# Attention values with a high|low stationary operand, and probabilities normalised before they are turned

## The chip, the cores and the metric

One NeuronCore of a Trainium2 chip runs the whole program. The metric is the device time of one execution in microseconds (us). The engines are PE (matmuls; PEld is its weight load), DVE (VectorE), ACT (ScalarE), POOL (GpSimd) and SP (DMA queues). Each works through its own instructions in order, and semaphores join them.

## What is computed

A network in float32 over 256 latent and 256 context tokens, 1024 features wide. The first block has two layers, each a mixer (attention beside a state-space scan, SSD) and a feed-forward part; layer 0 also updates the context, layer 1 only the latents. The second block has a layer of sparse attention by an index (DSA) with a feed-forward part, and a layer with three attention branches (NSA: compressed keys, selected blocks, a window) with eight experts. The attention of the first block reads:

```python
def one_block(q_blk):
    s = jnp.einsum('bqkgd,bskd->bkgqs', q_blk, k).astype(jnp.float32) * scale
    p = jax.nn.softmax(s, axis=-1).astype(v.dtype)
    return jnp.einsum('bkgqs,bskd->bqkgd', p, v)
```

Heads have 64 features; in the first block 8 query heads share 2 key heads, in the second 16 share 4. DSA and NSA add masks, and NSA adds up its branches, each times a gate by token and head. The attended heads, beside the scan's output in the first block, go through an output projection.

## The kernel before

The program is one long stream: the first block's layers, then DSA, then NSA. Linear layers hold each operand as a high part and a rest, both float32r, and add three products (`mm3`, L369 to L371; the weights are split by ACT at L363 and DVE at L364). Features lie along the partitions of `hT` and `mixT` (two parts, high and low), 128 tokens to a tile. A scheduler orders each engine's instructions by priority, and the written order sets the priority; pools of tiles with a fixed number of buffers (`bank("tr", 2)` for transposes, `bank("o", 2)` for the attention's outputs, `wk` for work tiles) add waits.

Attention goes by groups of one token tile (L627 to L672): 1 head with 512 keys, 2 heads with 256, or 4 heads with 128. Layer 0 has 24 groups (16 of 512 keys, 8 of 256), layer 1 has 16 of 512, DSA 12 (4 of 128 keys, 8 of 256), NSA 24 (8 of 128, 16 of 256) and four compressed steps. A group has three steps:

- `scores`: the matmuls against the keys (L643, L644; L639 adds a mask), DVE's maximum (L647), ACT's Exp with the row sums (L652), one for each head.
- `turn`: four transposes of the probabilities on PE (L660) and one copy out of PSUM (`evac`, two of three by ACT at L130, one by DVE at L132).
- `values`: float32 matmuls (L670) with the turned probabilities of 128x128 as stationary operand and 64 columns of V moving. Their output has tokens along the partitions, eight heads of 64 in one bank.

After eight heads DVE takes the reciprocal of the row sums and multiplies the bank by it (`heads_out`, L1245; in NSA also the gates, and L1248 and L1249 add the branches). `to_mixT` then turns the 512 features with four transposes (L680), DVE copies them out (L685), ACT casts the high part (L691) and DVE subtracts (L692). A block of eight heads and one token tile is a job; there are four in layer 0, two in layer 1, four in DSA and four in NSA: 14.

`pipeline(units, (1, 2))` writes the steps of DSA and NSA so that a group's `turn` comes one group after its `scores`, its `values` two more after that, and what follows `values` with it. In the mixers the groups are merged with the scan and the convolutions. In NSA the compressed branch (`compressed`) has its own scores (L1562, L1563), and its values are one float32 matmul of 512 columns (L1582) against a block-diagonal `vbd` that DVE makes at the entry by four products of 128x256 (L1503).

## Time and profile before

| | us |
|---|---|
| median of 3 runs | 2746.94 |
| lowest and highest | 2740.97, 2750.49 |
| the profiled execution | 2753.68 |
| its span in the trace | 2751.8 |
| PE busy | 2644.2 (96%) |
| DVE busy | 2100.7 (76%) |
| ACT busy | 1529.1 (56%) |
| POOL busy | 52.7 (2%) |

The granted TensorE clock over the span is 0.978 of full speed. The attention stages lie at about 100 to 267 us (layer 0), 830 to 916 (layer 1), 1230 to 1272 (DSA) and 1591 to 1680 (NSA). A busy share is an average over the span, so a stage is read from its own window. Ends of matmuls are modelled: what a matmul costs PE is read from one start to the next.

### The profile page before, as it was taken

What the parts mean: (1) busy time and instruction counts of PE and PEld (TensorE: products, weight loads), DVE (VectorE), ACT (ScalarE), POOL (GpSimd) and SP (SyncE); (2) the same over time, 40 slices, a digit from 0 to 9 for tenths busy, and PEclk for the clock granted to TensorE, in tenths of its full rate; (3) what the DMA queues carried; (4) which work ended last, traced back from release to release, by engine and by line L of the source; (5) the groups of instructions that cost most, each with busy time, mean ns of one, the idle gap of its engine ahead of it and who ended that gap; (6) DMA issues with size and microseconds to landing.
All of it is one profiled execution on the core that took longest, in us unless ns stands there. A gap on an engine that the chain in (4) does not pass through costs nothing. (4 is left out here: it accounts for less than half of the span.)

```text
span 2751.8 us, 37805 instructions
## 1 busy us (share of the span) xinstructions
PE 2644.2 (96%) x13941; PEld 2178.2 (79%) x13941; DVE 2100.7 (76%) x2818; ACT 1529.1 (56%) x2259; POOL 52.7 (2%) x103
## 2 busy tenths in 40 slices
PE   7999999999999899999999999999999999999998
PEld 4877777778777799778997888788888888787876
DVE  5777667566687777576765866899989898888887
ACT  4444532223554444465444654777777777777775
POOL 0011000000001000000000000000000000000000
PEclk9999999999999999999999998999999999999999
DMA  6321667776531388442875623899999999999996
GB/s 240 118 93 32 214 201 249 256 261 212 160 114 39 100 300 281 150 140 92 277 243 168 207 75 126 292 336 345 338 336 340 345 335 343 350 345 347 349 340 239
DMA packets 180264, 641.87 MB, mean 233 GB/s; under 512 B 20621, under 2 KB 21351, under 8 KB 180071
## 3 DMA queue, kind: packets, MB, share of 16 engines
q1 hardware_dynamic: 177840, 636.05, 66.4%
q10 hardware_dynamic: 2231, 3.33, 0.4%
q8 instruction: 111, 1.82, 0.3%
q14 instruction: 82, 0.67, 0.1%
HBM read 638.25 MB, written 1.05 MB: 232 GB/s over the span
## 5 line engine op out<-in xcount | busy, mean ns | idle before, releaser
L363 ACT CAST hl<-raw 128x1024 fp32r<-128x1024 f32 (+3 forms) x1010 | 1025.4, 1033 | 647.5 <-PE mm L371 391.1
L364 DVE TENSOR_TENSOR hl<-raw,hl 128x1024 fp32r<-128x1024 f32 (+3 forms) x1010 | 1184.2, 1200 | 204.3 <-ACT hl L363 198.8
L370 PE MATMUL mm<-hl,h 128*128 128x512 f32 (+4 forms) x1616 | 631.5, 391 | 4.0 <-DVE hl L364 3.1
L371 PE MATMUL mm<-hl,h 128*128 128x512 f32 (+4 forms) x1616 | 626.3, 388 | 0.0
L369 PE MATMUL mm<-hl,h 128*128 128x512 f32 (+4 forms) x1616 | 623.8, 389 | 1.1 <-DVE wk L1160 0.8
L369 PE MATMUL mm<-h,hl 128*128 128x256 f32 (+1 forms) x1208 | 394.5, 327 | 6.0 <-DVE hl L364 5.9
L370 PE MATMUL mm<-h,hl 128*128 128x256 f32 (+1 forms) x1208 | 391.2, 324 | 0.0
L371 PE MATMUL mm<-h,hl 128*128 128x256 f32 (+1 forms) x1208 | 390.9, 324 | 0.0
L370 PEld LDWEIGHTS mm<-hl,h 128*128 128x128 f32 x1616 | 304.8, 189 | 77.9 <-DVE hl L364 13.3
L369 PEld LDWEIGHTS mm<-hl,h 128*128 128x128 f32 x1616 | 304.9, 189 | 69.8 <-ACT hl L363 3.0
L371 PEld LDWEIGHTS mm<-hl,h 128*128 128x128 f32 x1616 | 304.8, 189 | 61.4
L296 DVE SCALAR_TENSOR_TENSOR mv<-mv,st 128x1024 f32<-128x1024 f32 x154 | 196.5, 1283 | 109.9 <-DMA mv<-in_w_ada_dram 76.0
L369 PEld LDWEIGHTS mm<-h,hl 128*128 128x128 f32 x1208 | 228.2, 189 | 35.1 <-DVE hl L364 10.8
L371 PEld LDWEIGHTS mm<-h,hl 128*128 128x128 f32 x1208 | 228.0, 189 | 21.1 <-issue 1.7
L370 PEld LDWEIGHTS mm<-h,hl 128*128 128x128 f32 x1208 | 228.2, 189 | 20.5 <-issue 1.7
L370 PE MATMUL o<-hl,h 128*128 128x512 f32 x480 | 191.5, 399 | 1.4 <-DVE hl L364 0.2
L371 PE MATMUL o<-hl,h 128*128 128x512 f32 x480 | 189.1, 394 | 0.0
L369 PE MATMUL o<-hl,h 128*128 128x512 f32 x480 | 178.9, 399 | 0.0
L370 PEld LDWEIGHTS o<-hl,h 128*128 128x128 f32 x480 | 90.3, 188 | 24.7 <-DVE hl L364 4.4
L369 PEld LDWEIGHTS o<-hl,h 128*128 128x128 f32 x480 | 90.2, 188 | 20.7 <-issue 0.8
L371 PEld LDWEIGHTS o<-hl,h 128*128 128x128 f32 x480 | 90.3, 188 | 19.6
L652 ACT ACTIVATE wk<-mm,nmx 128x256 f32<-128x256 f32 (+2 forms) x144 | 69.1, 491 | 55.6 <-DVE nmx L647 55.4
(448 smaller groups left out, 2801.4 us busy)
## 6 DMA issues: line engine op xcount, KB each, us to landing
raw<-in_moe_w_up_dram SPq DMA_DIRECT2D x221, 512.0 KB, 5.4
raw<-in_moe_w_gate_dram SPq DMA_DIRECT2D x220, 512.0 KB, 5.5
raw<-in_moe_w_down_dram SPq DMA_DIRECT2D x219, 512.0 KB, 5.2
mv<-in_w_ada_dram SPq DMA_DIRECT2D x96, 512.0 KB, 4.9
mv<-in_w_mod_dram SPq DMA_DIRECT2D x85, 512.0 KB, 4.6
raw<-in_w_gate_dram SPq DMA_DIRECT2D x44, 512.0 KB, 4.8
raw<-in_w_up_dram SPq DMA_DIRECT2D x44, 512.0 KB, 4.6
raw<-in_w_down_dram SPq DMA_DIRECT2D x44, 512.0 KB, 3.6
```

The costliest lines, as they stand in the source:

```text
L296: nc.vector.scalar_tensor_tensor(acc, raw, st[:, k, cnd:cnd + 1], acc, op0=ALU.mult, op1=ALU.add)
L363: self.in_turn("hi", lambda: nc.scalar.copy(hl[:, 0], raw), after and after[0])
L364: self.in_turn("lo", lambda: nc.vector.tensor_sub(hl[:, 1], raw, hl[:, 0]), after and after[1])
L369: nc.tensor.matmul(out, s[1], m[0], start=start, stop=False)
L370: nc.tensor.matmul(out, s[0], m[1], start=False, stop=False)
L371: nc.tensor.matmul(out, s[0], m[0], start=False, stop=stop)
L652: nc.scalar.activation(pr[:, j * nk:(j + 1) * nk], sb[:, j * nk:(j + 1) * nk], AF.Exp, bias=nmx[:, j:j + 1], accum_out=sm[:, g + j:g + j + 1])
```

## The change

V is stored once as a high part and a rest side by side, 64 + 64 columns of float32r (`vS`, made by `put_values`: ACT casts, DVE subtracts). This pair is now the stationary operand. The probabilities are normalised straight after the Exp: DVE takes the reciprocal of the row sums (and in NSA multiplies it by the gates, which are made ready once), and ACT scales each head by it (L667), or GpSimd all four heads where there are 128 keys (L663). After the transposes ACT casts the high part (L679) and DVE subtracts the rest (L680). The matmuls (L689) let the two parts of the probabilities move past V's pair, 256 columns at a time (512 where there are 128 keys). The output has features along the partitions: the rows of V's high part and those of its rest, which `heads_to_mixT` adds for four heads at a time (ACT copies at L703 and L704, DVE adds at L705 and L706, ACT casts at L708, DVE subtracts at L709). The transposes and copies of `to_mixT` go for attention, as do `heads_out` and the norms.

A job now fills two banks "o" of four heads each where it filled one of eight; in NSA all branches add into these two in PSUM, from the compressed values to the last branch. The compressed values are eight matmuls of 128 columns against `vst`, made by four products of 128x512. The lag is (2, 2), and in layer 1 `n_head` is 5 where it was 7.

```diff
+    def put_values(self, dst, src):
+        self.nc.scalar.copy(dst[:, :, 0], src)
+        self.nc.vector.tensor_sub(dst[:, :, 1], src, dst[:, :, 0])
...
+            nc.vector.reciprocal(sm, sm)
+            if coef is not None:
+                nc.vector.tensor_mul(sm, sm, coef[:, g:g + hb])
+            if hb > 2:
+                nc.gpsimd.tensor_mul(pr.rearrange("p (h k) -> p h k", h=hb), pr.rearrange("p (h k) -> p h k", h=hb),
+                                     sm.unsqueeze(2).to_broadcast([128, hb, nk]))
+            else:
+                for j in range(hb):
+                    nc.scalar.activation(pr[:, j * nk:(j + 1) * nk], pr[:, j * nk:(j + 1) * nk], AF.Copy, scale=sm[:, j:j + 1])
 
         def turn():
...
-            pt = self.wk(512)
-            self.evac(pt[:, :hb * nk], tb[:, :hb * nk])
-            st["pt"] = pt
+            if g % vb == 0:
+                sh["pT"] = pool.tile([128, 2, nkt, vb, 128], F32R, name="pT", bufs=2)
+            src = tb.rearrange("p (h k n) -> p k h n", h=hb, k=nkt)
+            hi, lo = (sh["pT"][:, i, :, g % vb:g % vb + hb] for i in range(2))
+            st["pT"] = sh["pT"]
+            nc.scalar.copy(hi, src)
+            nc.vector.tensor_sub(lo, src, hi)
 
         def values():
-            pt, ob = st["pt"], o_of()
-            for j in range(hb):
-                for kt in range(nkt):
-                    c = (j * nkt + kt) * 128
-                    nc.tensor.matmul(ob[:, (g + j) * 64:(g + j + 1) * 64], pt[:, c:c + 128],
-                                     v_of(g + j, kt), start=(kt == 0), stop=(kt == nkt - 1))
+            if (g + hb) % vb:
+                return
+            g0 = g + hb - vb
+            out = o_of(g0)[:, (g0 % 4) * 128:(g0 % 4 + vb) * 128]
+            for kt in range(nkt):
+                for i in (1, 0):
+                    nc.tensor.matmul(out, v_of(g0, kt), st["pT"][:, i, kt].rearrange("p h n -> p (h n)"),
...
+    def heads_to_mixT(self, mixT, k0, t, ob):
...
+        nc.scalar.copy(s[lo], ov[hi, :, 0])
+        nc.scalar.copy(s[hi], ov[lo, :, 1])
+        nc.vector.tensor_add(f[lo], ov[lo, :, 0], s[lo])
+        nc.vector.tensor_add(f[hi], ov[hi, :, 1], s[hi])
+        h, l = (mixT[:, i, k0:k0 + 2, t * 128:t * 128 + 128] for i in range(2))
+        nc.scalar.copy(h, f)
+        nc.vector.tensor_sub(l, f, h)
...
-            n_head = 7 if last else 5
+            n_head = 5
...
-            self.pipeline(units, (1, 2))
+            self.pipeline(units, (2, 2))
...
+                    v2 = self.wk(2, 64).bitcast(F32R)
+                    nc.scalar.copy(v2[:, 0], b[:, h * 64:h * 64 + 64])
+                    nc.vector.tensor_sub(v2[:, 1], b[:, h * 64:h * 64 + 64], v2[:, 0])
+                    nc.vector.tensor_mul(vst[:, h], v2.bitcast(F32).rearrange("p a d -> p (a d)").unsqueeze(1).to_broadcast([128, 4, 128]),
+                                         rowm.unsqueeze(2).to_broadcast([128, 4, 128]))
...
                         def values():
-                            ob = self.bank("o", 2)
-                            nc.tensor.matmul(ob, st["pT"], vbd[:, hf], start=True, stop=True)
...
+                            for g in range(2):
+                                for h in range(4):
+                                    nc.tensor.matmul(o_of(4 * g)[:, h * 128:h * 128 + 128], vst[:, 2 * hf + g, h], st["pT"][:, g],
+                                                     start=(h == 0), stop=False, skip_group_check=True)
```

On ACT, in the second half of DSA (groups of 256 keys; `wk` are probabilities, `tr` the transposed ones in PSUM, `h` is `mixT`), before:

```order
L652 ACTIVATE wk,sums<-mm,nmx 128x256 x2
L130 COPY wk<-tr 128x512
L652 ACTIVATE wk,sums<-mm,nmx 128x256 x2
L130 COPY wk<-tr 128x512
L691 CAST h<-wk 128x4x128
L652 ACTIVATE wk,sums<-mm,nmx 128x256 x4
L691 CAST h<-wk 128x4x128
L130 COPY wk<-tr 128x512
```

and after, where `psum` holds the reciprocals, `pT` the turned parts and `o` the output bank:

```order
L704 COPY wk<-o 64x256
L657 ACTIVATE wk,psum<-mm,nmx 128x256 x2
L708 CAST h<-wk 128x2x128
L667 ACTIVATE wk<-wk,psum 128x256
L679 CAST pT<-tr 128x512
L667 ACTIVATE wk<-wk,psum 128x256
L703 COPY wk<-o 64x256
L704 COPY wk<-o 64x256
```

A group had an Exp for each of its two heads and a copy in two of three cases. It now has the Exps, two scalings (L667) and the cast (L679), and the copies out of the output bank (L703, L704) with their cast (L708) stand in between.

On PE, at the end of DSA, the last values (L670), the transposes of `to_mixT` (L680) and the first output projection (L369 to L371), before:

```order
L670 MATMUL o<-h,wk 128x64 x2
L660 MATMUL tr<-cons,wk 128x128 x2
L670 MATMUL o<-h,wk 128x64 x2
L680 MATMUL tr<-cons,wk 128x128 x4
L670 MATMUL o<-h,wk 128x64 x5
L321 MATMUL mm<-cons,moda_189 128x128 x5
L680 MATMUL tr<-cons,wk 128x128 x4
L321 MATMUL mm<-cons,moda_189 128x128
L369 MATMUL mm<-hl,h 128x512
L370 MATMUL mm<-hl,h 128x512
```

and after:

```order
L673 MATMUL tr<-cons,wk 128x128 x4
L689 MATMUL o<-pT,vS 128x256 x4
L371 MATMUL mm<-hl,h 128x512
L369 MATMUL mm<-hl,h 128x512
L370 MATMUL mm<-hl,h 128x512
L371 MATMUL mm<-hl,h 128x512
L689 MATMUL o<-pT,vS 128x256 x8
L369 MATMUL mm<-hl,h 128x512
L370 MATMUL mm<-hl,h 128x512
```

The transposes of `to_mixT` are gone, and matmuls of the output projection for the first token tile stand between the last transposes (L673) and values (L689); 18 of them stand ahead of the last eight of L689.

On DVE, in layer 0 among the scan's products (L988, L1021, L1002), before:

```order
L1245 TENSOR_TENSOR wk<-o,rsum 128x512
L1020 TENSOR_TENSOR de<-ec,d 128x8
L647 TENSOR_REDUCE nmx<-mm 128x2
L685 COPY wk<-tr 128x512
L1021 TENSOR_TENSOR wk<-h,de 128x512
L1002 TENSOR_TENSOR qy<-qy,o 128x512
L692 TENSOR_TENSOR h<-wk,h 128x4x128
L132 COPY wk<-tr 128x512
L1020 TENSOR_TENSOR de<-ec,d 128x8
L647 TENSOR_REDUCE nmx<-mm 128x2
```

and after, where L652 is the maximum and L1055 and L1054 are the scan's products:

```order
L705 TENSOR_TENSOR wk<-o,wk 64x256
L706 TENSOR_TENSOR wk<-o,wk 64x256
L652 TENSOR_REDUCE nmx<-mm 128x2
L709 TENSOR_TENSOR h<-wk,h 128x2x128
L680 TENSOR_TENSOR pT<-tr,pT 128x512
L1055 TENSOR_TENSOR wk<-h,de 128x512
L659 RECIPROCAL psum<-psum 128x2
```

The product with the row sums (L1245) and the copy (L685) are gone; each group has a subtraction (L680) and a reciprocal (L659), and the heads have sums of 64x256 (L705, L706).

## Rows read from the trace of the kernel before

**Rows 1.** The page, busy time of each engine over the span (share, instructions).

```profile
PE 2644.2 (96%) x13941; PEld 2178.2 (79%) x13941; DVE 2100.7 (76%) x2818; ACT 1529.1 (56%) x2259; POOL 52.7 (2%) x103
```

**Rows 2.** Windows (from:to, length, busy time (count) by engine, clock, DMA): layer 0, 1, DSA, NSA.

```profile
100.00:265.00 165.00, 159.61 (x928) 123.41 (x927) 117.14 (x187) 74.67 (x157) 19.16 (x30) 0.99 0.25 84
830.00:900.00 70.00, 63.12 (x369) 51.95 (x367) 51.22 (x82) 31.19 (x63) 9.21 (x14) 0.90 0.13 38
1230.00:1271.00 41.00, 36.06 (x280) 32.93 (x278) 25.82 (x48) 27.19 (x90) 0.00 (x0) 0.92 0.08 27
1591.00:1680.00 89.00, 85.42 (x643) 78.95 (x643) 57.57 (x135) 50.38 (x177) 0.00 (x0) 0.92 0.17 61
```

**Rows 3.** Groups by line and shape (busy, mean ns, idle before): the values' matmuls.

```profile
L670 PE MATMUL o<-h,wk 128*128 128x64 f32 x416 | 55.6, 276 | 2.3 <-ACT wk L130 2.3
L670 PE MATMUL o<-kv,wk 128*128 128x64 f32 x192 | 25.0, 268 | 0.0
```

**Rows 4.** PE's timeline in DSA (start, length, instruction): scores and values.

```profile
1250.15 0.28 PE L644 MATMUL mm<-kSb,qS 128*128 128x256 f32 x1
1250.27 1.00 PE L670 MATMUL o<-h,wk 128*128 128x64 f32 x8
1251.08 0.48 PE L639 MATMUL mm<-mask,identr 128*128 128x512 f32 x1
```

**Rows 5.** PE's timeline at the end of DSA: the transposes of to_mixT, the output projection.

```profile
1267.68 0.61 PE L680 MATMUL tr<-cons,wk 128*128 128x128 f32 x4
1268.12 1.23 PE L670 MATMUL o<-h,wk 128*128 128x64 f32 x10
...
1270.93 0.48 PE L369 MATMUL mm<-hl,h 128*128 128x512 f32 x1
1271.25 0.39 PE L370 MATMUL mm<-hl,h 128*128 128x512 f32 x1
1271.48 0.40 PE L371 MATMUL mm<-hl,h 128*128 128x512 f32 x1
```

**Rows 6.** Groups by line and shape: ACT's scalings, exponentials, copies and casts.

```profile
L652 ACT ACTIVATE wk<-mm,nmx 128x256 f32<-128x256 f32 x64 | 29.9, 478 | 21.8 <-DVE nmx L647 21.7
L1338 ACT ACTIVATE wd<-cons,ik 128x128 f32<-128x128 f32 x16 | 5.2, 394 | 0.0
L826 ACT ACTIVATE wk<-wk,cols 128x512 f32<-128x512 f32 x14 | 11.4, 813 | 0.0
L130 ACT COPY wk<-tr 128x512 f32<-128x512 f32 x52 | 30.5, 587 | 21.8 <-PE tr L660 21.7
L612 ACT CAST wk<-h 128x256 fp32r<-128x256 f32 x20 | 7.2, 420 | 0.0
```

**Rows 7.** Groups by line and shape: subtractions of DVE, the product of GpSimd.

```profile
L1799 DVE TENSOR_TENSOR h<-tr,h 128x512 fp32r<-128x512 f32 x56 | 38.4, 686 | 9.2 <-ACT h L1798 9.2
L692 DVE TENSOR_TENSOR h<-wk,h 128x512 fp32r<-128x512 f32 x20 | 14.7, 733 | 1.6 <-ACT h L691 1.4
L975 POOL TENSOR_TENSOR wk<-ad,cons 128x512 f32<-128x512 f32 x24 | 27.0, 1127 | 75.5 <-PE o L995 24.2 <-PE mm L978 20.9 <-DVE h L835 11.0
```

**Rows 8.** Windows: the two halves of DSA, the second part of NSA.

```profile
1231.00:1251.00 20.00, 15.29 (x103) 13.07 (x102) 12.54 (x24) 13.64 (x51) 0.00 (x0) 0.83 0.14 49
1251.00:1271.00 20.00, 19.76 (x173) 18.98 (x172) 12.72 (x24) 12.70 (x39) 0.00 (x0) 1.00 0.01 2
1640.00:1676.00 36.00, 35.99 (x301) 34.05 (x300) 24.08 (x51) 23.35 (x77) 0.00 (x0) 1.00 0.16 60
```

**Rows 9.** The entry of NSA: a window, and two rows of DVE's timeline.

```profile
1593.00:1598.00 5.00, 2.26 (x13) 1.98 (x13) 4.54 (x12) 2.00 (x5) 0.00 (x0) 0.84 0.93 333
...
1591.60 0.42 DVE L1503 TENSOR_TENSOR h<-mm,cons 128x256 f32<-128x256 f32 x1 [0.52 <-PE mm L1499]
...
1604.25 0.20 DVE L1584 RECIPROCAL csums<-csums 128x8 f32<-128x8 f32 x1
```

**Rows 10.** PE's timeline at the beginning of DSA: the wait for the first Exp.

```profile
1237.02 0.80 PE L639 MATMUL mm<-mask,identr 128*128 128x512 f32 x1 [3.82 <-ACT wk L652]
```

More of the change, by code (lines that the diff above doesn't have):

```diff
@@ L619, in query_stack, with attention, attention_group @@
         return qS
[L621 to L633 removed]
+    def put_values(self, dst, src):
+        self.nc.scalar.copy(dst[:, :, 0], src)
+        self.nc.vector.tensor_sub(dst[:, :, 1], src, dst[:, :, 0])
+    def attention(self, H, nk, pool, q_of, k_of, v_of, mask, coef, o_of, bounds, finish):
+        hb = max(1, min(H, 512 // nk))
+        st = {}
+        return [self.attention_group(g, hb, nk, pool, st, q_of, k_of, v_of, mask, coef, o_of, bounds, finish)
+                for g in range(0, H, hb)]
+    def attention_group(self, g, hb, nk, pool, sh, q_of, k_of, v_of, mask, coef, o_of, bounds, finish):
+        nc = self.nc
+        nkt = nk // 128
+        vb = max(2, hb)
         st = {}
@@ L726, in block1_mixer @@
             q_sb = [None] * 4
-            kv = part(4, 256)
+            vS = big.tile([128, 4, 2, 2, 64], F32R, name="vS")
+            hst = part(2, 512)
+            kk_ = big.tile([128, 4, 128], F32, name="kk")
             zs = part(4, 512)
@@ new lines, in dsa, with att_job, o_of @@
+                units += self.att_job(big, mixT, t, hf, lambda h, n=n: stacks[n][:, h], lambda n=n: prep(n + 1),
+                                      [(kS, vS, masks[t], None)])
+            self.pipeline(units, (2, 2))
+        return mixT
+    def att_job(self, pool, mixT, t, hf, q_of, prep, branches, first=None):
+        banks = {}
+        def o_of(g):
+            if g // 4 not in banks:
+                banks[g // 4] = self.bank("o", 2)
+            return banks[g // 4]
+        units = [] if first is None else [first(o_of)]
+        for b, (kS, vS, mask, coef) in enumerate(branches):
+            units += self.attention(
+                8, 128 * (t + 1), pool, q_of,
+                lambda h, kS=kS: (kS[0][:, 2 * hf + h // 4, :128 * (t + 1)], kS[1][:, 2 * hf + h // 4, :128 * (t + 1)]),
+                lambda h, kt, vS=vS: vS[:, kt, 2 * hf + h // 4].rearrange("p a d -> p (a d)"), mask, coef, o_of,
+                (b == 0 and first is None, b == len(branches) - 1),
+                lambda g, ob: self.heads_to_mixT(mixT, 4 * hf + g // 2, t, ob))
@@ L1574, in turn @@
+                            nc.vector.tensor_mul(pr, pr, cs.unsqueeze(2).to_broadcast([128, 8, 16]))
+                            st["p2"] = p2 = self.wk(2, 2, 64).bitcast(F32R)
+                            pv = pr.rearrange("p (g h) n -> p g (h n)", g=2)
+                            nc.scalar.copy(p2[:, :, 0], pv)
+                            nc.vector.tensor_sub(p2[:, :, 1], pv, p2[:, :, 0])
                         def turn():
                             tb = self.bank("tr", 2)
-                            nc.tensor.transpose(tb[:, 0:128], st["pr"].rearrange("p h n -> p (h n)"), self.ident)
@@ new lines, in turn @@
+                            st["pT"] = self.wk(2, 128).bitcast(F32R)
+                            nc.scalar.copy(st["pT"], tb[:, 0:256].rearrange("p (g n) -> p g n", g=2))
+                        def values():
+                            for g in range(2):
+                                for h in range(4):
+                                    nc.tensor.matmul(o_of(4 * g)[:, h * 128:h * 128 + 128], vst[:, 2 * hf + g, h], st["pT"][:, g],
+                                                     start=(h == 0), stop=False, skip_group_check=True)
@@ new lines, in compressed @@
+                        return [scores, turn, values]
+                    return self.att_job(big, mixT, t, hf, lambda h: stacks[n][:, h], lambda: prep(n + 1),
+                                        [(kS[i], vS[i], self.causr[:, 128 - 128 * t:256], gv[:, i]) for i in (1, 2)], compressed)
+                nc.vector.tensor_scalar(gt, gt, 0.5, 0.5, op0=ALU.mult, op1=ALU.add)
+                for t in tl:
+                    g0 = gt[:, t].rearrange("p (h b) -> p b h", b=3)[:, 0]
+                    nc.vector.tensor_scalar(g0, g0, cons[:, C_ROWM + t:C_ROWM + t + 1], None, op0=ALU.mult)
```

145 lines of the change are left out of this document (48 added, 97 removed).

## The prediction, made before a run of the changed kernel

> **What bounds the kernel now.** I read the page's busy times first: PE is busy for 96% of the span [rows 1], so the first question is how much PE time the change removes, and the second which engine takes over where it does. The edit only touches four attention stages, so the next view is the busy time in those four windows [rows 2]. They hold 365 us, and PE is the fullest engine in each: 159.6 of 165, 63.1 of 70, 36.1 of 41 and 85.4 of 89 us. DVE follows in the two mixers (117.1 and 51.2 us), while in DSA and NSA ACT stands at 27.2 and 50.4 us. Everything outside these windows (feed-forwards, experts, modulation) keeps its instructions, and I count it at nothing.
>
> I measure against the profiled execution, 2753.7 us around a span of 2751.8 us. It lies 6.8 us above the median of 2746.94 us. The sum below is a difference, worked out on that execution and then put on the median.
>
> **What PE saves.** Line 670 has 416 + 192 records [rows 3]: 76 groups of eight, two records for each float32 matmul of 64 columns. A group's eight begin at 1250.27 and the next matmul begins at 1251.08 [rows 4]: 0.81 us. In their place stand float32r matmuls like the scores', of which one of 256 columns takes 0.12 us from start to start [rows 4] and one of 512 columns 0.23 us [rows 5]. A group with 256 or 512 keys gets four of 256 columns (0.48 us), a group with 128 keys two of 512 (0.46 us). Each group saves 0.33 us, in all 76 x 0.33 = 25 us. The four transposes of to_mixT, 0.44 us [rows 5], go for each of 14 blocks of eight heads: 6 us. The compressed values trade one 512-column float32 matmul for a second transpose and eight matmuls of 128 columns, which I leave at nothing. By stage this is 24 x 0.33 + 4 x 0.44 = 9.7 us in layer 0, 6.2 in layer 1, 5.7 in DSA and 9.7 in NSA: 31 us.
>
> Could the old form be cheap after all? A 64-column record takes 0.10 us, a 256-column float32r matmul 0.12 us [rows 4]. Paid by columns alone, the eight records' 512 columns would take 0.24 us; they take 0.81, so something other than columns is paid for, and it is paid per record. I take the rows' saving; that a group of the new form costs 0.8 us as well is a rival below. The Trainium skill (FP8 and Floating Point Precision, section TensorE Precision Notes) has a rule that speaks for this rival: true FP32 makes four passes through the array, reduced FP32 reads the same 4 bytes cut short. By that rule four matmuls of 64 columns are as many columns as four of 256, the values save nothing, and the sum would be 25 us worse; the trace shows two records for each matmul.
>
> **What ACT and DVE get.** ACT scales each head. The nearest rows are a Copy with a scale vector on 128 columns, 5.2 us for 16 = 0.33 us, an Exp with a bias vector on 256, 29.9 / 64 = 0.47 us, and a scaled 512 columns, 0.81 us [rows 6]. For 256 columns I take 0.45 us, nearest to the Exp (0.33 to 0.81); for 512 columns 0.7 us (0.47 to 0.81). ACT also takes every cast out of PSUM, where it took two of three copies: a third of 0.59 us [rows 6], 0.2 us. So a group of 256 keys costs ACT 2 x 0.45 + 0.2 = 1.1 us more, one of 512 keys 0.9 us, one of 128 keys 0.2 us, since there GpSimd scales (its 128x512 product takes 1.13 us [rows 7], beside the other engines but in the chain of its group). Every four heads get two copies of 64x256 and a cast of 256 columns; at the price of a 256-column cast, 0.36 us [rows 6], that is 1.08 us, against half of a 512-wide cast that goes.
>
> DVE subtracts for every group: the same form (PSUM minus SBUF into float32r) took 38.4 / 56 = 0.69 us [rows 7]. With a reciprocal of 0.2 us [rows 9] and a third of the 0.69 us copies gone, that is +0.65 us a group. The heads roughly cancel: a product with the row sums, a copy and a subtraction of 512 go (three at about 0.7 us, as the last of them [rows 7]), four 64x256 sums and two subtractions of 256 come, six at 0.42 us [rows 9]: +0.4 us for eight heads.
>
> **Stage by stage.** In layer 0 DVE goes from 117 to about 134 us of 165 and ACT from 75 to about 105, PE from 160 to 150. PE stays the fullest, but a DVE at 86% of the shorter stage keeps it waiting more often. I take 6 of the 9.7 us: -6 (-10 to -2).
>
> In layer 1 sixteen groups put DVE at 51.2 + 16 x 0.65 + 0.8 = 62.4 us of 70, PE falls to 57. DVE becomes the fullest engine, with a chain of group after group. I take -2 (-6 to +3).
>
> In DSA the second half is the place. ACT is busy 12.7 of the 20 us from 1251 to 1271, which hold eight groups of 256 keys [rows 8]. It gets 8 x 1.1 us, some five blocks of four heads at 1.08 us, and loses three 512-wide casts at about 0.6 us: 12.7 + 8.8 + 5.4 - 1.8 = 25 us. ACT then needs 5 us more than the window has. Against this stands what PE can do meanwhile: before, the output projection starts at 1270.93, when the last transposes are through [rows 5]; in the changed order 18 of its 512-column matmuls stand between the last values, 18 x 0.23 = 4.2 us, and the casts behind that wait for ACT. Of the first half, which begins with a wait of 3.8 us for the first Exp [rows 10], nothing is won: the reciprocal, GpSimd's 1.13 us and the cast with its subtraction lengthen the first chain by some 2 us, which the longer lag covers in part, and four groups save 1.3 us of PE. I take 25 - 20 - 4.2 + 1 = +2 (-2 to +6).
>
> In NSA the same stands between 1640 and 1676: sixteen groups of 256 keys, ACT 23.4 us, PE 36.0 of 36 [rows 8]. ACT gets 16 x 1.1 + 4 x 1.08 - 1.2 = 20.7 us and needs 44 us, 8 more than PE did. Back come 8 x 0.33 = 2.7 us of PE saved in the groups of 128 keys before, and about 3 us by the woven projection, as in DSA. The entry gets four products of 512 in place of 256 (0.69 for 0.42 us), four more subtractions of 256 and four small ones: 1.1 + 1.7 + 0.8 = 3.6 us of a DVE that is busy nearly throughout from 1593 to 1598 [rows 9]; I count half, 1.8. Holding both output banks from a job's compressed values to its last branch is left at nothing, since the scores of later groups cover it; without this cover each of three changes of job costs a copy, a copy, two sums, some 1.6 us. Sum: 8 - 2.7 - 3 + 1.8 = +4 (-5 to +10).
>
> -6 - 2 + 2 + 4 = -2: 2746.9 - 2 = **2745 us**.
>
> **The rivals.**
> *PE's saving arrives* (chance 0.25). For it: PE is the fullest engine in all four windows, and ACT and DVE have idle time in each [rows 2]. Against it: ACT's sums in DSA and NSA. If the lag hides ACT, the stages give -9, -6, -3 and -5 us: -23, or 2724 us.
>
> *ACT sets the pace* (0.25, slower). The place is ACT's queue in DSA and NSA: Exp, scale, cast of the probabilities and the two head copies stand in one row, and PE's transposes wait for them. Waits cost twice, since the clock falls: in the half of DSA with the 3.8 us wait [rows 10] the granted clock is 0.83, in the other 1.00 [rows 8], so part of it ran at 1.2 instead of 2.4 GHz. From where does it decide? PE's pace now is 20 / 8 = 2.5 us a group in DSA and 36 / 16 = 2.25 in NSA [rows 8]; ACT's sum gives 3.1 and 2.75. If nothing weaves, DSA gives +5 and NSA +9; the mixers, with a longer chain, -2 and +2. That is +14, or 2761 us.
>
> *The change does not do what it says on PE* (0.04). If a group's values take 0.8 us in the new form too, only the transposes' 6 us are left, while ACT and DVE carry all they get: about -1, +2, +5 and +8 us, +14 together, or 2761 us. Against it stand the 0.12 us of the scores' matmuls, which have the same type and width [rows 4].
>
> *Part of the saving, part of ACT* (0.46), the forecast: 2745 us, with its own range from 2733 to 2755.
>
> **How the numbers follow.** About 0.3%, or 8.2 us, is what a measurement of this kernel can tell from no change: 2738.7 and 2755.2 are the limits. Of the forecast's 0.46 I put 0.07 below, 0.34 inside, 0.05 above; of the first rival's 0.25, 0.23 below and 0.02 inside; of the second's 0.25, 0.04 inside and 0.21 above; of the third's 0.04, 0.01 inside and 0.03 above. Faster 0.30, same 0.41, slower 0.29. The range reaches to the middle of the two outer rivals, 2726 to 2762 us, and leaves about a tenth on either side.
>
> **What would show it.** The group's values on PE should take 0.48 us from start to start; 0.8 would mean the third rival. ACT should be busy for 40 to 43 us in DSA and 72 to 76 in NSA, with PE's longest waits there on ACT's scale and cast lines. PE in the mixers should be 8 to 10 and 5 to 6 us less busy, with the stage shorter by some two thirds and one third of it. In NSA, PE's first compressed values of a job should not wait for the copies of the job before. I am wrong on the low side if DSA and NSA end earlier than now, because ACT runs ahead through the lag; on the high side if PE's clock stays low through DSA and NSA because of many short waits.

## The result: 72 us slower, some 30 us of it outside the attention

The changed kernel takes 2820.7 us (median of four runs, 2815.71 to 2823.99) against 2748.59 us for the kernel before. The ratio is 1.0259 [1.0242, 1.0277]: 72 us, or 2.6%, slower. The forecast of 2745 us and its whole range, 2726 to 2762 us, are missed. The profiled execution after took 2821.1 us, with a span of 2819.4 us.

The page after, busy time by engine; it answers to [rows 1]:

```profile
PE 2642.0 (94%) x13585; PEld 2160.1 (77%) x13585; DVE 2148.5 (76%) x2987; ACT 1616.4 (57%) x2472; POOL 64.9 (2%) x115
```

PE is busy for about as long as before, in a span that is 68 us longer. PE now waits, or runs at the lower clock. To see where, I cut both executions at the same PE instructions: the first matmul of a part's scores, the last values matmul, the first transposes of the feed-forward that follows. In us, worked out from PE's timelines of the profiled executions ("end of layer 1" runs from its last values matmul to the first transposes of the feed-forward behind it; "the rest" is all that is left, a good 2000 us, nearly all of it code that the change does not touch):

| part | before | after | after - before |
|---|---|---|---|
| layer 0, from the start | 312.9 | 322.6 | +9.7 |
| layer 1, to the last values | 157.8 | 164.4 | +6.6 |
| end of layer 1 | 32.6 | 69.9 | +37.3 |
| DSA | 66.5 | 75.7 | +9.2 |
| NSA | 76.1 | 97.7 | +21.6 |
| the rest | 2105.9 | 2089.1 | -16.8 |

The rest gives back 6.5 us in the feed-forward behind DSA and 7.3 us behind NSA's last values, where part of the output projection has already been done.

**The end of layer 1.** Windows (from:to, length, busy time by engine with counts, granted clock, DMA share, GB/s) of this place, before and after:

```profile
917.00:948.00 31.00, 24.77 (x115) 19.36 (x114) 18.39 (x30) 15.67 (x31) 2.31 (x4) 0.94 0.32 102
```

```profile
931.00:999.00 68.00, 29.72 (x108) 20.61 (x107) 35.70 (x44) 15.68 (x33) 2.31 (x4) 0.69 0.41 139
```

The new time holds hardly any PE work, but 17 us more of DVE. The timeline after (start, length, engine and line, [idle time before it, and what ended it]) names the work:

```profile
947.33 3.93 DVE L296 SCALAR_TENSOR_TENSOR mv<-mv,st 128x1024 f32<-128x1024 f32 x3 [3.92 <-DMA mv<-in_w_kv_ada_dram]
...
951.31 1.92 PE L300 MATMUL tr<-mv,ones 128*32 128x512 f32 x4 [12.75 <-DVE mv L296]
...
969.89 1.92 PE L300 MATMUL tr<-mv,ones 128*32 128x512 f32 x4 [16.66 <-DVE mv L296]
971.86 0.59 ACT L303 COPY wk<-tr 128x512 f32<-128x512 f32 x1 [32.22 <-PE tr L300]
...
973.98 0.70 POOL L1102 TENSOR_TENSOR rsy<-ssy,mhalf 128x2 f32<-128x2 f32 x1 [81.62 <-DVE ssy L1101]
974.71 0.28 DVE L1105 TENSOR_SCALAR wk<-cons,rsy 128x128 f32<-128x128 f32 x1 [0.81 <-POOL rsy L1102]
975.11 1.14 PEld L719 LDWEIGHTS tr<-wk,qy 128*128 128x128 f32 x5 [1.90 <-issue]
975.14 1.19 PE L719 MATMUL tr<-wk,qy 128*128 128x128 f32 x4 [1.53 <-DVE wk L1105]
```

L296 multiplies `in_w_kv_ada`, a modulation weight that only the second block needs. This product is filler: each late attention group of layer 1 carries `self.fill(0.3)`, and the credit of these calls opens step after step of generators that wait in a list. `n_head` sets which groups are late. With 7, nine of the sixteen groups carry the call, 2.7 steps; with 5, eleven do, 3.3 steps. The third whole step opens the next generator, the sixteen-step product with `in_w_kv_ada`. Behind the mixer `settle_fillers()` finishes whatever generator is open, all at once, ahead of the scan's output (L719, L1105). PE stands twice before L300, 12.75 and 16.66 us, because the weight's blocks still have to be loaded and multiplied one after the other. SP's queue was held as well, since the next load needs the buffer that L300 frees (waits: engine and line, what it waited for, us in total, times, longest):

```profile
SPq L253 <- PE tr L300: 52.2, 1, 52.2
```

**The attention stages.** Windows after, from layer 0 to NSA, then two pieces: the second half of DSA, and in NSA the first and the second half. The first, third and fourth answer to [rows 2]:

```profile
100.00:277.00 177.00, 158.20 (x846) 116.39 (x845) 134.62 (x240) 103.24 (x216) 18.47 (x30) 0.97 0.23 78
814.00:931.00 117.00, 99.84 (x543) 80.82 (x541) 90.74 (x162) 65.58 (x125) 9.31 (x20) 0.93 0.15 46
1279.00:1332.00 53.00, 42.14 (x225) 34.27 (x224) 35.62 (x73) 41.61 (x126) 4.41 (x4) 0.81 0.07 22
1644.00:1755.00 111.00, 99.40 (x562) 87.25 (x563) 65.02 (x175) 75.94 (x245) 8.36 (x8) 0.78 0.12 44
```

```profile
1315.00:1330.00 15.00, 12.06 (x79) 9.58 (x77) 10.88 (x24) 14.73 (x42) 0.00 (x0) 1.00 0.00 1
```

```profile
1650.00:1680.00 30.00, 28.87 (x125) 26.66 (x125) 13.37 (x39) 13.40 (x53) 4.18 (x4) 0.50 0.02 7
1705.00:1750.00 45.00, 39.89 (x254) 33.69 (x254) 27.83 (x81) 41.63 (x127) 0.00 (x0) 0.92 0.13 48
```

ACT is busy for 14.73 of 15 us in DSA's second half and for 41.63 of 45 us in NSA's: there it is the bound, where PE was [rows 8]. NSA's first half is another matter: PE is busy for 28.87 of 30 us, at a granted clock of 0.50, the lower level of 1.2 GHz. The whole first part of NSA, from its first scores to the first Exp of 256 keys, before and after:

```profile
1601.30:1637.90 36.60, 36.23 (x261) 33.59 (x261) 21.12 (x56) 20.61 (x85) 0.00 (x0) 0.86 0.01 2
```

```profile
1654.50:1702.70 48.20, 45.40 (x241) 42.01 (x242) 23.44 (x65) 23.12 (x92) 8.36 (x8) 0.66 0.00 1
```

A mean clock of 0.66 over 48.2 us is 33 us at the lower level, 0.86 over 36.6 us is 10 us.

In layer 0 no engine is full. Some of PE's waits in it, before (100 to 270) and after (100 to 280):

```profile
PE tr L841 <- ACT wk L130: 1.4, 1, 1.4
PE tr L660 <- ACT wk L652: 1.3, 3, 0.9
```

```profile
PE o L689 <- DVE pT L680: 5.6, 6, 2.4
PE tr L673 <- ACT wk L667: 4.2, 5, 1.9
PE mm L1047 <- DVE h L1073: 2.1, 2, 1.2
PE o L1029 <- DVE wk L1022: 1.4, 1, 1.4
```

The two largest waits are new, for the two steps that the change puts between a group's matmuls: the scaling (L667) and the subtraction (L680). The scan's matmuls (L1047, L1029, L1058) now wait for DVE too, 4.9 us in all, where before they did not.

### The profile page after: what moved, and what is told of

Same layout as the page of the kernel before. It is cut to its first block, busy times and chain, and to the rows that moved or that the text cites. A ratio compares the mean times of both kernels' runs of the same rounds, so it can differ in the third digit from the quotient of the medians.

```text
span 2819.4 us, 37516 instructions
## 1 busy us (share of the span) xinstructions
PE 2642.0 (94%) x13585; PEld 2160.1 (77%) x13585; DVE 2148.5 (76%) x2987; ACT 1616.4 (57%) x2472; POOL 64.9 (2%) x115
## 5 line engine op out<-in xcount | busy, mean ns | idle before, releaser
L369 PE MATMUL mm<-hl,h 128*128 128x512 f32 (+4 forms) x1616 | 624.2, 390 | 2.2 <-ACT grow L130 1.4
L371 PE MATMUL mm<-hl,h 128*128 128x512 f32 (+4 forms) x1616 | 625.6, 387 | 0.0
L369 PE MATMUL mm<-h,hl 128*128 128x256 f32 (+1 forms) x1208 | 393.6, 327 | 3.4 <-DVE hl L364 3.2
L371 PE MATMUL mm<-h,hl 128*128 128x256 f32 (+1 forms) x1208 | 391.2, 324 | 0.0
L369 PEld LDWEIGHTS mm<-hl,h 128*128 128x128 f32 x1616 | 304.9, 189 | 71.5 <-ACT hl L363 2.5
L371 PEld LDWEIGHTS mm<-hl,h 128*128 128x128 f32 x1616 | 304.8, 189 | 61.2
L296 DVE SCALAR_TENSOR_TENSOR mv<-mv,st 128x1024 f32<-128x1024 f32 x154 | 196.6, 1283 | 109.9 <-DMA mv<-in_w_ada_dram 73.6
L369 PEld LDWEIGHTS mm<-h,hl 128*128 128x128 f32 x1208 | 227.6, 189 | 30.8 <-DVE hl L364 6.4
L371 PEld LDWEIGHTS mm<-h,hl 128*128 128x128 f32 x1208 | 227.8, 189 | 21.0 <-issue 1.7
L371 PE MATMUL o<-hl,h 128*128 128x512 f32 x480 | 189.0, 394 | 0.0
L369 PE MATMUL o<-hl,h 128*128 128x512 f32 x480 | 179.0, 400 | 0.0
L369 PEld LDWEIGHTS o<-hl,h 128*128 128x128 f32 x480 | 90.2, 188 | 20.7 <-issue 0.8
L371 PEld LDWEIGHTS o<-hl,h 128*128 128x128 f32 x480 | 90.3, 188 | 19.6
```

The lines of the kernel that those rows point to most:

```text
L296: nc.vector.scalar_tensor_tensor(acc, raw, st[:, k, cnd:cnd + 1], acc, op0=ALU.mult, op1=ALU.add)
L369: nc.tensor.matmul(out, s[1], m[0], start=start, stop=False)
L371: nc.tensor.matmul(out, s[0], m[0], start=False, stop=stop)
```

## The experiments

Ratios are to the kernel before, run on the same chip. The five kernels with the same code in the mixers (after, and the experiments on n_head, on the lag of DSA and NSA, on scaling by DVE, and on float32 matmuls in the first experiment's kernel) differ by up to 6.4 us in layer 0 and 3.6 us in layer 1 of their profiles, so a few us in one part of one profile say nothing. The three with the same code in DSA and NSA (after, and the experiments on n_head and on the mixers' lag) differ by 0.7 us in DSA and 4.5 us in NSA. Where n_head is given back, the comparison is with the first experiment, 2790.8 us. That one ran on a chip where the kernel before takes 2745.43 us, later ones on chips where it takes up to 2749.71 us; a difference of two medians carries these 4 us, a difference of two ratios does not.

**n_head alone, from both sides.** Theory: the filler costs the 37 us at layer 1's end. Rival: the attention's longer chain does, and the filler only fills the gap.

```diff
-            n_head = 5
+            n_head = 7 if last else 5
```

> The changed kernel, but with n_head 7 in layer 1 as before, so that two units fewer advance the modulation's work between the attention's groups (0.3 of a step each). Theory (filler): with n_head 5 one more step is taken, which opens the modulation for NSA's keys, and the call that finishes an opened one then puts all its 15 remaining steps, with their loads, ahead of the scan's output of layer 1. With 7 it stays closed: the stretch from the last values of layer 1 to the first transposes of the feed-forward's entry, 69.9 us against 32.5 before, goes back to 32 to 35 us, some of it is given back in the later feed-forward that now runs the modulation (9 us at most), and the whole comes to 2784 to 2793 us. Rival (the new attention itself holds up layer 1's end, by its output banks or its longer chain): the stretch stays above 60 us and the time within 4 us of 2820.

Measured: 2790.84 us (2788.43 to 2800.32), ratio 1.0168 [1.014, 1.0196]; 30 us of the 72 are gone. The stretch is back at 30.2 us:

```profile
932.00:962.00 30.00, 23.89 (x114) 19.04 (x112) 18.31 (x30) 15.70 (x33) 2.31 (x4) 0.96 0.30 105
```

That is within the forecast of 2784 to 2793 us. The opposite edit in the kernel before (`n_head = 5`, nothing else):

> The kernel before, with n_head 5 in layer 1 as in the changed one, and nothing else. Theory (filler): the modulation for NSA's keys is opened here too, and the stretch behind layer 1's attention grows from 32.5 to about 70 us; the time comes to 2777 to 2786 us. Rival (it takes the new attention): 2748 us within 4, since only two units change their place.

Measured: 2772.26 us (2772.14 to 2778.74), ratio 1.0099 [1.0075, 1.0122], 27 us more, and 5 us under the range expected. The hole is there without any of the new attention:

```profile
910.00:976.00 66.00, 34.41 (x131) 24.38 (x130) 37.23 (x46) 16.82 (x33) 2.80 (x5) 0.72 0.43 143
```

The feed-forward behind DSA is 6.8 us shorter here too: the work done early is missing later, which is why a hole of 37 us costs about 30. The rival falls. What is left, 45 us, belongs to the rest of the change.

**The lag of DSA and NSA.** The first experiment with `(1, 2)` for `(2, 2)`:

> As e1_fill_as_before, with the lag (1, 2) of the kernel before in DSA and NSA. Theory (the chain of a group is longer, and the lag covers it): PE waits more for the scaled probabilities, 3 to 8 us slower than e1_fill_as_before. Rival (the longer lag only delays the transposes, and with them the release of buffers): 2 to 6 us faster than e1_fill_as_before.

Measured: 2788.5 us, ratio 1.0154 [1.0132, 1.0176], within 3 us of the first experiment. The lag neither hides nor costs anything that can be told here.

**Scaling by DVE.** In DSA and NSA, the groups of 256 keys:

```diff
-                    nc.scalar.activation(pr[:, j * nk:(j + 1) * nk], pr[:, j * nk:(j + 1) * nk], AF.Copy, scale=sm[:, j:j + 1])
+                    if hb == 2 and mask is not None:
+                        nc.vector.tensor_scalar(pr[:, j * nk:(j + 1) * nk], pr[:, j * nk:(j + 1) * nk], sm[:, j:j + 1], None, op0=ALU.mult)
+                    else:
+                        nc.scalar.activation(pr[:, j * nk:(j + 1) * nk], pr[:, j * nk:(j + 1) * nk], AF.Copy, scale=sm[:, j:j + 1])
```

> As e1_fill_as_before, but the groups of 256 keys in DSA and NSA are scaled by DVE, not by ACT: 48 instructions of 128x256, about 0.45 us each, move from one to the other. Theory (ACT sets the pace in the second parts of DSA and NSA, where it is busy 4.8 to 5.0 of each 5 us): 4 to 9 us faster than e1_fill_as_before. Rival (latency and PE's clock set the time, not ACT's load): within 3 us of e1_fill_as_before.

Measured: 2785.93 us, ratio 1.014 [1.0117, 1.0163], 5 us less by the medians, which by itself is not clear of the first experiment's interval; DSA -3.1 and NSA -5.1 us in the profile. The gain in NSA lies in its second part, from the first Exp of 256 keys to the last values: 45.1 us here, against 49.8 to 53.9 us in the six profiles in which ACT scales there. ACT is no longer full in it, and DVE nearly is:

```profile
1672.40:1717.50 45.10, 40.48 (x281) 34.83 (x281) 40.70 (x121) 34.94 (x108) 0.00 (x0) 1.00 0.14 49
```

ACT's scaling is part of the cost, and moving it to a DVE that is itself short of time brings a part of it back.

**No normalisation.** Reciprocal, gates and scaling are left out of the first experiment's kernel.

```diff
-            nc.vector.reciprocal(sm, sm)
...
-                    nc.scalar.activation(pr[:, j * nk:(j + 1) * nk], pr[:, j * nk:(j + 1) * nk], AF.Copy, scale=sm[:, j:j + 1])
```

> As e1_fill_as_before without the normalisation: no reciprocal, no gate product, no scaling by ACT or GpSimd, so the attention's output is not divided by its row sums. This takes 53 us of ACT, 13 of GpSimd and some 10 of DVE away, and shortens each group's chain by about 1 us. Theory (ACT's load and the chain set the pace): DSA from first scores to the entry of its feed-forward falls from 75.3 to 66 to 71 us, NSA from 97.8 to 84 to 92, layer 0 up to its feed-forward's entry from 326 to 314 to 320; the whole 18 to 30 us faster than e1_fill_as_before. Rival (clock in NSA, DVE in the mixers): NSA stays above 94 and layer 0 above 322, the whole less than 10 us faster.

Measured: 2765.21 us (2755.48 to 2768.98), ratio 1.0049 [1.0027, 1.0071]: 26 us less by the medians, 33 by the ratios. By part: layer 0 -11.7, layer 1 -0.6, DSA -7.4, NSA -9.6 us.

**No low part of the probabilities.** The subtraction L680 goes, and with it the half of the values' matmuls that read its result.

```diff
-            nc.vector.tensor_sub(lo, src, hi)
...
-                for i in (1, 0):
+                for i in (0,):
...
```

> As e1_fill_as_before with the high part of the probabilities alone: no subtraction behind the turn (76 times 0.69 us of DVE) and half of the values' matmuls, so the output has less precision. Theory (in the mixers DVE's added load and the subtraction at the end of each chain hold PE up): layer 0 falls from 326 to 315 to 321 us, layer 1 from its entry to its last values from 163.8 to 157 to 161; DSA and NSA, where ACT is full, gain 2 to 5 us each; the whole 12 to 25 us faster than e1_fill_as_before. Rival (DVE has room, and ACT and the clock decide): the mixers gain under 3 us, the whole under 8.

Measured: 2770.3 us (2766.23 to 2774.56), ratio 1.0079 [1.0055, 1.0104]: 20 us less by the medians, 24 by the ratios. By part: layer 0 -13.6, layer 1 -6.4, DSA -2.5, NSA +2 us. What of it is DVE's and what PE's, this run doesn't part.

**Both left out.**

> As e1_fill_as_before without the normalisation and without the low part (the output is not divided by the row sums, and has less precision): what is left of the change is PE's new form, ACT's casts and the sums of the heads. Theory (PE's saving is there, and was covered by what ACT and DVE got): layer 0 up to its feed-forward's entry falls to 303 to 309 us (312.9 before), layer 1 from its entry to its last values to 150 to 155 (157.8 before), DSA to 60 to 65 (66.5 before), only NSA stays above before's 76.1 at 82 to 90, because PE's clock is low there; the whole 2730 to 2750 us. Rival (the new form saves PE nothing that the program can use): layer 0 above 311, DSA above 66, the whole above 2755.

Measured: 2745.25 us (ten runs, 2738.64 to 2754.3), ratio 0.9989 [0.9972, 1.0006]. The two effects add up within what can be told: 26 + 20 = 46 us against 45.6 together by the medians, 33 + 24 = 57 against 49 by the ratios. Without both, the 45 us are gone. This does not show that the rest of the change is free: the run also leaves out half of the values' matmuls, PE is busy for 2615.4 us in it, 29 less than before, and none of that arrives. What stays in (halves of V side by side, 256 columns moving, heads added in two) is level with the kernel before; layer 0 and layer 1 are then 6.0 and 3.8 us shorter than before, NSA 7.3 us longer, in its first part:

```profile
1590.60:1637.10 46.50, 44.94 (x232) 42.75 (x233) 16.02 (x42) 22.94 (x92) 0.00 (x0) 0.61 0.00 1
```

**Longer lags in the mixers**, `(2, 3)` and `(2, 2)` for `(1, 3)` and `(1, 2)`:

> As e1_fill_as_before, with one group more between scores and turn in the mixers too (lags (2, 3) and (2, 2) instead of (1, 3) and (1, 2)). Theory (latency of the longer chain): PE's waits for the scaling go, layer 0 and layer 1 together 5 to 11 us faster. Rival (throughput of DVE and ACT, or buffers): within 3 us, or slower by up to 5.

Measured: 2791.73 us, ratio 1.015 [1.0126, 1.0173], no change. Layer 1 gains 6.6 us and layer 0 loses 5.

**All scaling by GpSimd** (L663 for every group):

> As e1_fill_as_before, but GpSimd scales the probabilities of every group, not only those of 128 keys: 53 us of ACT go, GpSimd gets 64 products of 128x512 at about 1.07 us. Theory (what costs is ACT's load, and the place of the scaling in ACT's queue): layer 0 up to its feed-forward's entry falls from 326 to 316 to 322 us, DSA from 75.3 to 69 to 73, NSA from 97.8 to 88 to 93; the whole 12 to 22 us faster than e1_fill_as_before. Rival (what costs is the length of a group's chain, which GpSimd makes no shorter): within 5 us of e1_fill_as_before.

Measured: 2789.63 us, ratio 1.0149 [1.0128, 1.017], no change. DSA -3.6 and NSA -6.3 us, but layer 1 +7.4 and layer 0 +3.8. The profile with the same mixers further below (GpSimd's scaling with float32 matmuls) has +7.4 in layer 1 again and -0.7 in layer 0, so only the first of the two holds. GpSimd's product takes longer than ACT's, and PE's waits in layer 1 (814 to 931) are led by it:

```profile
L663 POOL TENSOR_TENSOR wk<-wk,psum 128x512 f32<-128x512 f32 x76 | 82.6, 1088 | 384.5 <-DVE psum L659 241.4 <-DVE psum L661 105.7 <-DVE de L1054 21.0
```

```profile
PE tr L673 <- POOL wk L663: 6.1, 5, 3.7
PE tr L673 <- POOL wk L860: 3.6, 2, 2.8
```

The wait for the scaling is not what is new: over the whole of layer 1 it is 8.3 us here and 7.7 us in the first experiment, for ACT. New are 3.6 us for the convolution's GpSimd work (L860) and 1.4 us more for the scan's (L1009), which now stand in one queue with the scaling. The same edit helps where ACT is full and, in layer 1, hurts where it is not.

**The low clock in NSA.** Theory: the lighter values matmuls leave PE at 1.2 GHz, and float32 work would raise it. Four float32 matmuls of 64 columns, their result overwritten, are put ahead of each group of 128 keys:

```diff
+            if hb == 4:
+                for _ in range(4):
+                    nc.tensor.matmul(sb[:, 0:64], self.ident, self.cons[:, 0:64], start=True, stop=True)
```

In the first experiment's kernel:

> As e1_fill_as_before, with four float32 matmuls of 64 columns more at the head of each group of 128 keys (4 groups in DSA, 8 in NSA); they write a bank that the scores then overwrite, and are as much float32 work as such a group's values were before, 0.8 us. Theory (clock): with the float32 matmuls gone PE runs the first half of NSA back to back at 1.2 GHz (granted 0.50 from 1620 to 1645 us in e1_fill_as_before, against 1605 to 1610 before), since only small and quick work is left there; with them back the clock rises sooner, and in spite of up to 10 us more of PE work NSA from its first scores to its last values falls from 97.8 us to 82 to 92, the whole by 6 to 16 us. Rival (the clock is low because PE waits for ACT and DVE, not because of what it runs): NSA gets longer by up to 6 us, the whole stays level or is up to 9 us slower than e1_fill_as_before.

Measured: 2789.52 us (2780.87 to 2797.57), ratio 1.0154 [1.0123, 1.0185]. NSA is 6.7 us shorter in the profile, which is of the fastest of the runs; the median moves by 1 us, so the whole has gained nothing that can be told. The first part of NSA is nevertheless another one than after:

```profile
1620.90:1661.90 41.00, 39.02 (x281) 36.74 (x282) 23.34 (x66) 22.85 (x92) 8.36 (x8) 0.88 0.00 1
```

The same in the kernel without both steps, and in the one with GpSimd's scaling:

> As e10_no_norm_no_low with the four float32 matmuls of e5_old_load at the head of each group of 128 keys. Theory (clock): with ACT and DVE relieved, what is left over in NSA is the low clock in its first half; NSA falls by 4 to 12 us against e10_no_norm_no_low, with the first half at a clock of 0.8 or more. Rival: the clock rises as early without them, and they cost their own 5 to 9 us.

> GpSimd scales every group (e9_scale_pool), and the groups of 128 keys carry the float32 matmuls of e5_old_load. Theory (both costs are real and add up): 3 to 9 us faster than e9_scale_pool in NSA, the whole 2762 to 2774 us. Rival (only one of them counts): within 3 us of e9_scale_pool.

Measured: 2736.85 us, ratio 0.9963 [0.9939, 0.9987], with 85.5 us for NSA where the kernel without the added matmuls had 83.4; and 2788.26 us, ratio 1.015 [1.0128, 1.0171], with 83.9 us for NSA against 91.5. NSA's first part takes 50.0 us at a clock of 0.62 in the first and 41.1 us at 0.88 in the second. By this part, one for and one against; the whole is 8 us shorter in the first, by intervals that still overlap, and the same in the second.

So the question was put to the kernel before, with only its values made lighter: their operands rounded to float32r (a change in precision). V gets a tile of its own for it, filled by copies in two pieces, and the program's DMA scratch is set as in the changed kernel (`dynamic_dma_scratch_size=1024`), which no run tested by itself; nothing else of the attention is touched.

```diff
-            self.evac(pt[:, :hb * nk], tb[:, :hb * nk])
+            self.evac(pt[:, :hb * nk].bitcast(F32R), tb[:, :hb * nk])
...
-                    nc.tensor.matmul(ob[:, (g + j) * 64:(g + j + 1) * 64], pt[:, c:c + 128],
+                    nc.tensor.matmul(ob[:, (g + j) * 64:(g + j + 1) * 64], pt[:, c:c + 128].bitcast(F32R),
...
```

> The kernel before with float32r in place of float32 for the values (turned probabilities and V are written as float32r, V in a tile of its own, which makes eight copies in two pieces; the compressed values too). The output has less precision; ACT and DVE do what they did. 304 matmuls of two records each become 304 of one, so PE saves 20 to 35 us. Theory (clock): in NSA the lighter PE work keeps the clock at the lower level for 15 us or more of its first half, and NSA stays at 72 us or above (76.1 before) though PE has 8 to 11 us less to do; layer 0 gets 3 to 9 us shorter, layer 1 and DSA 1 to 5 each, the whole 2730 to 2742 us. Rival (what PE has to do decides, and the low clock in the changed kernel came from its waits): NSA falls to 65 to 70 us and the whole to 2718 to 2730.

Measured: 2723.94 us (2717.97 to 2729.63), ratio 0.9921 [0.99, 0.9942]: 23 us faster than before, and with it the fastest kernel here. Its values are 304 records where [rows 3] has 608:

```profile
L670 PE MATMUL o<-vr,wk 128*128 128x64 f32 x304 | 48.0, 274 | 2.3 <-ACT wk L130 2.3
```

NSA takes 66.0 us, so the rival's 65 to 70 us came and the theory's 72 or more did not: lighter values alone do not bring the low clock. Then the float32 matmuls on top:

> As e13_before_f32r_values with the four float32 matmuls of e5 at the head of each group of 128 keys. Theory (clock): the clock rises sooner, and NSA gets 2 to 8 us shorter than in e13_before_f32r_values. Rival (what PE has to do decides): NSA gets 4 to 6 us longer.

Measured: 2741.25 us (twelve runs, 2720.74 to 2748.78), ratio 0.9959 [0.9936, 0.9981]. The profiled execution has 84.0 us for NSA. The first half of NSA in the two kernels, without the float32 matmuls and with them:

```profile
1581.00:1611.00 30.00, 27.98 (x210) 26.58 (x209) 17.69 (x47) 19.46 (x81) 0.00 (x0) 0.88 0.03 13
```

```profile
1580.00:1630.00 50.00, 49.98 (x277) 48.74 (x277) 19.42 (x50) 21.04 (x84) 0.00 (x0) 0.62 0.00 1
```

The kernel with more float32 work stays at the low level for longer. NSA is 18 us longer, where the theory had it shorter and the rival had 4 to 6 us more. In two kernels the added matmuls went with a shorter first part, in two not: the theory falls as a rule, and no other has taken its place.

What the profiles do show is where the low stretch belongs. In all nine of the new attention without added matmuls (after, and the experiments on n_head, lag, scaling, normalisation and low part), NSA's first part takes 46.5 to 52.3 us at clocks of 0.60 to 0.69. In the two of the old attention in float32 (before, and before with `n_head = 5`) it takes 36.6 and 36.0 us, both at 0.86, and in the one with rounded values 33.1 us at 0.90. So among kernels without added matmuls it goes with the change and not with one execution, and neither the normalisation nor the low part brings it, since it stays without them. That the old attention can have it too shows only in the last run, with 49.8 us at 0.62.

## Why the prediction was wrong

**"Everything outside these windows (...) keeps its instructions, and I count it at nothing": the largest miss.** The diff holds `n_head = 5`, which I noted among the changes and never priced. It changes no attention work, only how many times `fill` is called; I should have counted the calls (9 x 0.3 against 11 x 0.3) and asked what the third step opens. About 30 of the 72 us, shown from both sides.

**PE's saving: the price right, the busy time not.** A group's values begin at 1324.29 and the next matmul at 1324.83, 0.54 us for four, where 0.48 was predicted and 0.81 stood before [rows 4].

```profile
1324.29 0.70 PE L689 MATMUL o<-pT,vS 128*128 128x256 f32 x4
1324.83 0.39 PE L370 MATMUL mm<-hl,h 128*128 128x512 f32 x1
```

That is 76 x 0.27 = 21 us instead of 25. The third rival, that a group costs 0.8 us in the new form too, falls with these rows. So does the four-pass rule of the Trainium skill as I had applied it (FP8 and Floating Point Precision, section TensorE Precision Notes): four matmuls of 256 columns take less time here than four float32 ones of 64. PE's busy time follows only in part. Layer 0 from 100 us on and layer 1 to the last values, each before and after:

```profile
100.00:312.90 212.90, 207.03 (x1178) 158.21 (x1177) 148.70 (x240) 98.73 (x202) 22.74 (x36) 0.99 0.32 107
100.00:322.60 222.60, 201.62 (x1060) 147.17 (x1059) 162.72 (x288) 126.82 (x261) 22.04 (x36) 0.98 0.30 103
757.70:915.50 157.80, 143.86 (x818) 119.64 (x819) 120.95 (x249) 72.71 (x143) 10.44 (x25) 0.92 0.21 65
765.40:929.80 164.40, 140.61 (x770) 115.26 (x771) 132.09 (x287) 90.15 (x177) 10.60 (x25) 0.92 0.23 75
```

That is 5.4 and 3.3 us less, where 8 to 10 and 5 to 6 were to show it; in NSA's first part PE is busy for 45.4 us where it was for 36.2, at the lower clock.

**The prices of single instructions: right.** Groups by line and shape after (busy, mean ns of one, idle time before it), priced from [rows 6] and [rows 7]:

```profile
L667 ACT ACTIVATE wk<-wk,psum 128x256 f32<-128x256 f32 x64 | 29.5, 512 | 1.5 <-DVE psum L659 1.4
L667 ACT ACTIVATE wk<-wk,psum 128x512 f32<-128x512 f32 x32 | 23.1, 722 | 9.7 <-DVE psum L659 9.5
L663 POOL TENSOR_TENSOR wk<-wk,psum 128x512 f32<-128x512 f32 x12 | 12.8, 1064 | 109.4 <-DVE psum L661 81.9 <-DVE psum L659 22.3 <-PE mm L649 5.2
L680 DVE TENSOR_TENSOR pT<-tr,pT 128x512 fp32r<-128x512 f32 x76 | 52.1, 687 | 14.9 <-ACT pT L679 13.8
```

29.5 / 64 = 0.46 us (taken: 0.45), 0.72 (0.7), 1.06 (1.13), 0.69 (0.69). ACT has 41.6 us in DSA (40 to 43 forecast) and 75.9 in NSA (72 to 76).

**Layer 0 (-6 predicted, +9.7) and layer 1 (-2, +6.6): the step from busy time to time failed.** I took two thirds and one third of PE's saving because PE stayed the fullest engine. But the added steps lie between one matmul of a group and the next. PE's waits in layer 0 (100 us to the end) add up to 20.6 us after and 5.7 before; 14.9 more of waiting and 5.4 less of work make the 9.7 us. The two steps' waits are 9.8 us of it, and each of the two steps, left out, shortens layer 0 by 12 and 14 us. DVE's share, which I had looked at, was sized well (134.6 us, about 134 forecast), and it did cost: the 4.9 us that the scan's matmuls wait for DVE.

In layer 1 the same count gives 23.7 us of waiting against 14.0 and 3.3 us less work, which makes 6.4 of the 6.6 us. The largest two of the waits, neither of which stood before:

```profile
PE mm L991 <- DVE h L875: 5.9, 1, 5.9
PE tr L673 <- ACT wk L667: 5.3, 3, 2.8
```

Leaving out the low part brings 6.4 us and the normalisation 0.6. Without the normalisation L667's wait is gone, but others, of 4.2 us for the convolution's DVE work and 3.0 us for the Exp, stand in its place. The reading of [rows 2] was wrong here too: the sixteen groups run from 805 to 916, and I put their DVE work into a window of 70 us. Over the whole run of groups DVE goes from 80.6 us (807 to 917, before) to 90.7 us (814 to 931, after, shown above), and PE stays the fullest with 99.8.

```profile
807.00:917.00 110.00, 102.54 (x583) 84.09 (x583) 80.64 (x129) 48.15 (x94) 9.62 (x20) 0.93 0.11 34
```

**DSA (+2 predicted, +9.2) and NSA (+4, +14 with what the projection gives back): right mechanism in the second parts, two terms wrong.** I cut both stages at the first Exp of 256 keys (1249.5 before and 1301.7 after in DSA, 1637.9 and 1702.7 in NSA). NSA's second part is 9.9 us longer, where ACT's sum said 8, and 7.3 us come back behind it, where I had credited 3 for weaving. These steps held. Its first part, though, takes 48.3 us instead of 36.6, where I had counted 2.7 us of saving: that is the stretch at a clock of 0.50, and a low clock was only named at the end, as a way to be wrong, without a price. It was named there as the effect of many short waits; in the 30 us at 0.50 PE waits for 1.1. Some 23 us more at half the speed hold 11 us less of work, by an estimate from the two rows of this part: most of what the first part lost. In DSA the second part is 6.5 us longer. ACT's 5 us came, the 4.2 us credited against them for the woven projection did not. The first part is 2.7 us longer, 1 was predicted. PE's longest waits in DSA are

```profile
PE mm L644 <- ACT wk L657: 5.3, 3, 3.8
PE o L689 <- ACT wk L657: 1.5, 2, 0.8
```

so the engine is the one named, but the line is the Exp, which stands in one row with scales, casts and copies, and not one of those themselves; and 3.8 us of it, for the first Exp, were there before [rows 10]. In NSA PE's waits for the scaling come to 1.0 us, and it has none for the probabilities' cast (L679).

**Both banks held in NSA, "left at nothing":** one wait of 1.9 us for the heads of the job before. Small, but not nothing.

```profile
PE o L1613 <- DVE wk L706: 1.9, 1, 1.9
```

**The rivals.** "ACT sets the pace" (2761 us) named the right engine for the second parts of DSA and NSA, and is still 30 us short of the first experiment, since it left the mixers almost even. "PE's saving arrives" is what the kernel before does when only its values get cheaper and nothing is added: four records take 0.36 us there instead of eight in 0.81, 76 x 0.45 = 34 us, and 23 us of them arrive.

## What stays open

What in the change makes NSA's first half run at 1.2 GHz for so long. It is not the normalisation, the low part or the lighter values alone, and the amount of float32 work on PE does not settle it. The pieces that no run tested are the compressed values' new form, the two output banks held through a job and the 512 columns moving at 128 keys. The clock also differs between executions of one program: the last kernel, with rounded values and float32 matmuls, spreads over 28 us, with mean clocks over the whole from 0.974 to 0.983, the fastest runs at the higher ones; in which stages it differs, one profile cannot show. The figures by part rest on one profiled execution each, the totals on medians.

## What to carry to other kernels

Price every constant of a diff, and above all those that only steer work: a number that moves background work across a step's boundary can cost more than the work that the change is about. Where PE is the fullest engine of a stage, a saving on PE can be lost to steps that are put between one of its matmuls and the next; count the steps in the chain of a group before the busy shares. And look for the cheaper half of an idea: here lighter values matmuls without the new steps around them win 23 us, at lower precision.

## What the runs showed of the hardware

PE can be busy nearly without a break and still be granted the lower clock: 28.87 of 30 us at 0.50 after, and 49.98 of 50 us at a mean of 0.62 in the last experiment. A float32r matmul's time grows by far less than its columns in this range, by half for four times the columns: four of 64 columns take 0.36 us from start to start in the kernel with rounded values (1239.84 to the next matmul at 1240.20), four of 256 columns 0.54 us after.

```profile
1239.84 0.53 PE L670 MATMUL o<-vr,wk 128*128 128x64 f32 x4
1240.20 0.47 PE L639 MATMUL mm<-mask,identr 128*128 128x512 f32 x1
```
